# Four load buffers for three modulation vectors, and a rest in the steps that build the first gate

## The chip, the cores and the metric

The kernel runs on one core of a Trainium2 chip. The metric is the device time of one execution in microseconds (us); less is better. The engines are named as in the profile: PE (matrix engine), PEld (its weight loads), DVE (vector), ACT (scalar), POOL (GpSimd) and SP, whose queue issues every load of this kernel.

## The reference, cut to what matters

The kernel is one decoder layer for 512 tokens of width 1024: a modulated norm, an input projection, two groups of attention heads, an output projection, and an MLP. Six vectors of 1024 numbers modulate it:

```
mod = c @ w_ada + b_ada
sh1, sc1, gt1, sh2, sc2, gt2 = split(mod, 6)
h = rms_norm(x, g_pre_mix) * (1 + sc1) + sh1
o = attention(h @ w_in) @ w_out
x = x + gt1 * rms_norm(o, g_post_mix)
h = rms_norm(x, g_pre_ffn) * (1 + sc2) + sh2
x = x + gt2 * rms_norm(square(relu(h @ w_up)) @ w_down, g_post_ffn)
```

The change concerns gt1 (in the kernel the first gate, tiles `wv_g1`, `vs_g1`), sc2 (`a2`) and sh2 (`sh2`). Each is a vector of 1024 times a 1024 by 1024 block of `w_ada`, 4 MB. The trace leaves digits out of names, so `wv_g` is `wv_g1` there. gt2 is made elsewhere, in another way.

## The kernel before, in words

The program is one stream of steps, fully unrolled. It first computes sh1 and sc1 from `w_ada` (tiles `wm`, `macc`) while the first two column blocks of the input projection run (`pA`, `pB`, to about 81 us of the trace). Then come the other projections in chunks D, C and E (`pj_D`, `pj_C`, `pj_E`), with rotation, stacking and transposing of each piece (`ra`, `sk`, `skp`), the indexer scores (`ix`, `rl`, `wk`), the rounds that pick the top keys on DVE (`topk_round`, L571), and the compressed keys (`kcp`, `hid`). After that twelve units of attention run with the output projection (`op`) between them, and from 387 us the MLP (`up`, `dn`).

Side work is placed by the table PLAN (L41): a list of steps with the entry (t0, dt) is spread evenly over the slots t0 to t0+dt, step q of n at t0 + (q+0.5)/n*dt. Slot n is written into the program behind the n-th piece of main work (L850), so the slot of a step fixes its rank. Piece n of the main work includes one chunk of the projection: C0 to C3 stand in pieces 9 to 12.

Rank is not the order on the engines. The framework's scheduler lays every engine's instructions out when the program is built: it plays the program through its own time model and lets an engine take a step of lower rank when those of higher rank aren't ready. A tile with a tag takes one of the tag's buffers and holds it until its last reader is done; a step whose buffer isn't free isn't ready. On the chip each engine, and SP's queue of loads, then works strictly in the order laid out.

`vec_steps` (L710) makes one vector: 8 loads of 512 KB (tag "vw", two buffers), 8 steps `mm(i)` on PE of four small matmuls each (the trace shows eight), and after every fourth a `finish`. A load needs the buffer that an earlier `mm` gives back. The four `mm` of one half add into one PSUM bank `vs`, held until `finish` has read it; banks of the tag "S" (four) also serve the projection's pieces and the indexer scores. For the first gate `finish` (L746) adds the bias tile `bb` on DVE, spreads it over the partitions on PE (`gv_g`) and multiplies on DVE. `bb` is one of six buffers of the tag "m2", which rotation, stacking and indexer tiles use too. Its result is first read by the output projection, in slot 25. The vectors a2 and sh2 have slots 25 to 27 and 29 to 32.

Of the kernel before, what the change touches and what calls it, by code (L numbers as in the profile page):

```python
# [9 lines left out]
F32 = mybir.dt.float32  # L10
# [7 lines left out]
P = 128  # L18
# [27 lines left out]
    x22=(32.6, 0.1), h22=(33.35, 1.68), x23=(33.6, 0.1), sD=(0, 0.48), cl=(0.2, 4.48), lC=(0.5, 0.1),  # L46
    sC=(3.7, 2.94), lE=(8.2, 0.1), sE=(8.3, 5.379), ix=(8.2, 5.88), cpe=(10, 0.1), ck1=(11.1, 1.077),
    cv1=(13.2, 0.784), ck2=(11.7, 2.8), ck3=(15, 2.8), cv2=(14.6, 0.98), cv3=(15.2, 1.05), tk1=(13, 6),
    g1=(6, 8),
)  # L50
UNITS = [("s", 0), ("w", 0), ("s", 1), ("w", 1), ("d", 0), ("d", 1),
         ("s", 2), ("w", 2), ("d", 2), ("s", 3), ("w", 3), ("d", 3)]
# [17 lines left out]
def layer_kernel(  # L70
# [6 lines left out]
    nc = tc.nc  # L77
# [3 lines left out]
    big = ctx.enter_context(tc.tile_pool(name="big", bufs=1))  # L81
    sml = ctx.enter_context(tc.tile_pool(name="sml", bufs=1))
    psp = ctx.enter_context(tc.tile_pool(name="psp", bufs=2, space=PSUM))

    N_U, N_RAW, N_B4, N_K, N_P, N_M = 10, 4, 9, 6, 7, 6

    def ht(tag, name, dt=F32R):
        return big.tile([P, NT, KT, P], dt, tag=tag, name=name, bufs=1)
# [16 lines left out]
    def m2(name, dt=F32):  # L105
        return big.tile([P, 512], dt, tag="m2", name=name, bufs=N_M)
# [5 lines left out]
    def bank(tag, name, dt=F32):  # L112
        return psp.tile([P, 512], dt, tag=tag, name=name, bufs=4 if tag == "S" else 2)
# [426 lines left out]
    def Q2(nm, t):  # L540
        rv = heads(pjs[nm, t], 8)
        sks[nm, t] = [stack(rv[:, g * 4:g * 4 + 4, :], 4, f"{nm}{t}{g}", G) for g in range(2)]

    def Q3(nm, t):
        q = b4(f"q{nm}_{t}", F32R).rearrange("p (h q) -> p h q", q=P)
        for g in range(2):
            ps = stack_T(sks[nm, t][g], 4, f"{nm}{t}{g}")
            A.copy(q[:, g * 4:g * 4 + 4, :], ps.rearrange("p (h q) -> p h q", q=P))
        (qn if nm == "C" else qd)[t] = q
# [113 lines left out]
    none = lambda *a: None  # L663
# [43 lines left out]
                V.scalar_tensor_tensor(acc[:, sl], ps, ROOT_D, gb[:, sl], op0=OP.mult, op1=OP.mult)  # L707
        return seq + [fin]

    def vec_steps(c0, nm, finish):  # L710

        stt = {}

        def load(i):
            stt[i] = big.tile([P, 4, 256], F32, tag="vw", name=f"wv_{nm}{i}", bufs=2)
            n, q = divmod(i, 2)
            SY.dma_start(stt[i], wa[:, 4 * q:4 * q + 4, c0 + n * 256:c0 + n * 256 + 256])

        def mm(i):
            half, n, q = i // 4, i // 2 % 2, i % 2  # L720
            if i % 4 == 0:
                stt["ps"] = bank("S", f"vs_{nm}{half}")
            for j in range(4):
                PE.matmul(stt["ps"][32 * j:32 * j + 32, n * 256:n * 256 + 256],
                          c_sb[:, 4 * q + j:4 * q + j + 1].to_broadcast([P, 32]), stt[i][:, j, :],
                          start=(q == 0), stop=(q == 1))
            if i % 4 == 3:
                finish(half, stt["ps"])
        nv = 2
        seq = [lambda i=i: load(i) for i in range(nv)] + [none] * 6  # L730
        for i in range(8):
            seq.append(lambda i=i: mm(i))
            if i + nv < 8:
                seq.append(lambda i=i: load(i + nv))
        return seq

    def g1_steps(c0, gvec):
        bb = {}

        def begin():  # L740
            res["g1"] = big.tile([P, 1024], F32, tag="g1", name="g1", bufs=1)
            SY.dma_start(res["g1"], gvec.to_broadcast([P, D]))
            for half in range(2):
                bb[half] = m2(f"bb_{half}")
                SY.dma_start(bb[half], b_ada[0:1, c0 + half * 512:c0 + half * 512 + 512].to_broadcast([P, 512]))

        def finish(half, ps):
            g = res["g1"][:, half * 512:half * 512 + 512]
            V.scalar_tensor_tensor(bb[half], bb[half], 0.25, ps, op0=OP.mult, op1=OP.add)
            pg = bank("S", f"gv_g1{half}")  # L750
            PE.matmul(pg, ones, bb[half], start=True, stop=True)
            V.tensor_tensor(g, pg, g, op=OP.mult)
        return [begin] + vec_steps(c0, "g1", finish)

    def col_steps(c0, nm):
        dst = cst.tile([P, KT], F32, name="col_" + nm)

        def finish(half, ps):
            acc = m2(f"acc_{nm}{half}")
            A.copy(acc, ps)  # L760
            pc = bank("S", f"cv_{nm}{half}")
            for k in range(4):
                PE.matmul(pc[:, k:k + 1], acc[:, k * P:(k + 1) * P], ones[:, 0:1], start=True, stop=True)
            h = half * 4
            V.scalar_tensor_tensor(dst[:, h:h + 4], pc[:, 0:4], 1.0 / 32.0,
                                   colT[:, c0 // P + h:c0 // P + h + 4], op0=OP.mult, op1=OP.add)
        return dst, vec_steps(c0, nm, finish)
# [19 lines left out]
    for f in lD:  # L787
# [4 lines left out]
            lambda t, nm=nm: Q2(nm, t), lambda t, nm=nm: Q3(nm, t)), t) for t in range(NT) for nm in "C"]  # L792
    tl += tD + tC
    ix = [(t, h) for t in range(1, NT) for h in range(4)]
    tk = {t: topk_steps(t) for t in range(1, NT)}
    g1s = g1_steps(2 * D, g_post_mix)
    a2, a2s = col_steps(4 * D, "a2")
    sh2, sh2s = col_steps(3 * D, "sh2")
# [39 lines left out]
    for n in range(len(tl) + 3):  # L838
# [5 lines left out]
        while mm_done < min(want, len(mm_seq)):  # L844
            f, t = tl[mm_seq[mm_done]]
# [290 lines left out]
    def finish(t, half):  # L1136
        hs = [slice(i * 512, i * 512 + 512) for i in range(2)]
        jk = m2(f"fj_{t}{half}")
        A.activation(jk, yacc[t][:, hs[half]], AF.Square, accum_out=sy[t][:, half:half + 1])  # L1139
        V.tensor_tensor(yacc[t][:, hs[half]], yacc[t][:, hs[half]], res["g2"][:, hs[half]], op=OP.mult)  # L1140
        if half == 1:
            rs = st([P, 1], "ro")
            rstd_of(rs, sy[t])
            for i in range(2):
                V.scalar_tensor_tensor(yacc[t][:, hs[i]], yacc[t][:, hs[i]], rs, x2[t][:, hs[i]],
                                         op0=OP.mult, op1=OP.add)
                SY.dma_start(ov[t][:, hs[i]], yacc[t][:, hs[i]])
# [58 lines left out]
```

## Time and profile before

| what | us |
|---|---|
| median of 3 runs | 737.91 |
| lowest and highest of them | 736.64, 738.00 |
| the profiled execution's own time | 736.85 |
| its span, first to last instruction | 735.1 |

The span is what the trace covers; 1.75 us lie around it. Row times count from the start of the span. A wait in brackets is the idle time of that engine just before the row, with what ended it. PEclk, the granted clock, has two levels: 1.00 is 2.4 GHz and 0.50 is 1.2 GHz; over a stretch it is a mean.

### The profile page before, as it was taken

How to read it: one execution, taken by the hardware profiler on the slowest of the kernel's cores; microseconds unless marked ns; L12 is line 12 of the kernel's file. 1: busy time of each engine (PE TensorE's matmuls, PEld its weight loads, DVE VectorE, ACT ScalarE, POOL GpSimd, SP SyncE). 2: the span in 40 equal slices, each digit the busy share in tenths (PEclk: the TensorE clock that was granted, in tenths of full speed). 3: DMA queues.
4: the chain of work that ended last, by engine and by line, in shares of the span. 5: the costliest groups of instructions: out<-in, count | busy, mean ns of one | idle time of the engine just before them, and what ended most of it. 6: DMA issues, size and time to landing. Idle time of an engine off the chain costs nothing.

```text
span 735.1 us, 9839 instructions
## 1 busy us (share of the span) xinstructions
PE 686.9 (93%) x3473; PEld 541.7 (74%) x3473; DVE 485.3 (66%) x1014; ACT 341.8 (46%) x715; POOL 160.5 (22%) x223
## 2 busy tenths in 40 slices
PE   3878997999999999899999999999999999999995
PEld 2656885777766576565698888888888888788884
DVE  5997644979999988885586464653735445443547
ACT  6654584624788569554475313322331332323222
POOL 4673084535623243321020000000000000000003
PEclk9998998969979999999999999999999999999998
DMA  8985643170004580462131352533325133231202
GB/s 268 325 267 151 190 112 119 57 173 1 2 1 132 164 221 8 135 230 83 51 98 58 98 168 107 160 127 115 126 65 183 58 114 115 78 123 58 86 1 114
DMA packets 67610, 87.13 MB, mean 119 GB/s; under 512 B 3973, under 2 KB 38889, under 8 KB 67562
## 3 DMA queue, kind: packets, MB, share of 16 engines
q1 hardware_dynamic: 67562, 86.52, 38.0%
q8 instruction: 27, 0.44, 0.2%
q14 instruction: 21, 0.17, 0.1%
HBM read 84.40 MB, written 2.10 MB: 118 GB/s over the span
## 4 chain that ended last, share of the span: by engine, by line
PE 75%; DVE 14%; DMA 3%; issue 3%; ACT 2%; POOL 1%; SPq 0%; POOLq 0%; DVEq 0%; ACTq 0%
PE up L1119 23%; PE dn L1160 22%; PE op L1012 6%; PE O L911 3%; PE pj_E L323 2%; DVE macc L289 2%; PE pA L323 2%; PE pj_D L323 2%; PE pj_C L323 2%; PE tp_s L905 1%; DMA x<-in_x_dram 1%; PE pB L323 1%; PE tp_w L905 1%; PE hid_v L628 1%; DMA wv_g<-in_w_ada_dram 1%
## 5 line engine op out<-in xcount | busy, mean ns | idle before, releaser
L1119 PE MATMUL up<-hh,uh_U 128*128 128x512 f32 (+1 forms) x288 | 104.6, 366 | 0.7 <-ACT hh L123 0.7
L1119 PE MATMUL up<-hh,ul_U 128*128 128x512 f32 (+1 forms) x288 | 104.9, 366 | 0.0
L1119 PE MATMUL up<-hl,uh_U 128*128 128x512 f32 (+1 forms) x288 | 104.0, 366 | 0.0
L1160 PE MATMUL dn<-uh_D,al 128*128 128x512 f32 x256 | 99.6, 389 | 0.0
L1160 PE MATMUL dn<-uh_D,ah 128*128 128x512 f32 x256 | 98.7, 391 | 0.0
L1160 PE MATMUL dn<-ul_D,ah 128*128 128x512 f32 x256 | 98.5, 389 | 0.0
L203 POOL TENSOR_SCALAR ms<-sy 128x1 f32<-128x1 f32 x4 | 3.6, 911 | 341.6 <-ACT fj L1139 341.6
L124 DVE TENSOR_TENSOR ul_D<-rw_D,uh_D 128x1024 fp32r<-128x1024 f32 (+1 forms) x35 | 41.3, 1181 | 47.5 <-ACT uh_D L123 45.4
L1166 DVE TENSOR_TENSOR y<-dn,y 128x512 f32<-128x512 f32 x56 | 38.3, 689 | 50.3 <-PE dn L1160 50.3
L1123 ACT ACTIVATE rl<-up 128x512 f32<-128x512 f32 x32 | 19.1, 598 | 92.7 <-PE dn L1160 59.2
L1119 PEld LDWEIGHTS up<-hh,uh_U 128*128 128x128 f32 x288 | 54.3, 188 | 9.7 <-ACT hh L123 0.9
L1119 PEld LDWEIGHTS up<-hh,ul_U 128*128 128x128 f32 x288 | 54.3, 189 | 8.8
L1119 PEld LDWEIGHTS up<-hl,uh_U 128*128 128x128 f32 x288 | 53.7, 189 | 8.9 <-DVE hl L124 0.2
L123 ACT CAST uh_U<-rw_U 128x1024 fp32r<-128x1024 f32 x32 | 33.7, 1052 | 55.1 <-PE dn L1160 51.9
L123 ACT CAST uh_D<-rw_D 128x1024 fp32r<-128x1024 f32 (+1 forms) x36 | 36.3, 1010 | 49.5 <-PE up L1119 37.5
L1160 PEld LDWEIGHTS dn<-uh_D,al 128*128 128x128 f32 x256 | 48.1, 188 | 10.2 <-issue 0.2
L1160 PEld LDWEIGHTS dn<-uh_D,ah 128*128 128x128 f32 x256 | 48.0, 188 | 10.2 <-issue 0.2
L1160 PEld LDWEIGHTS dn<-ul_D,ah 128*128 128x128 f32 x256 | 48.0, 188 | 10.0
L124 DVE TENSOR_TENSOR ul_U<-rw_U,uh_U 128x1024 fp32r<-128x1024 f32 x32 | 39.1, 1222 | 11.9 <-ACT uh_U L123 10.9
L1124 DVE TENSOR_TENSOR rl<-rl 128x512 f32<-128x512 f32 x32 | 22.1, 690 | 34.8 <-ACT rl L1123 34.8
L123 ACT CAST ah<-rl 128x512 fp32r<-128x512 f32 x32 | 19.8, 620 | 29.3 <-DVE rl L1124 29.3
L124 DVE TENSOR_TENSOR al<-rl,ah 128x512 fp32r<-128x512 f32 x32 | 22.0, 689 | 11.0 <-ACT ah L123 11.0
(409 smaller groups left out, 1558.7 us busy)
## 6 DMA issues: line engine op xcount, KB each, us to landing
rw_U<-in_w_up_dram SPq DMA_DIRECT2D x32, 512.0 KB, 4.7
rw_D<-in_w_down_dram SPq DMA_DIRECT2D x32, 512.0 KB, 3.5
wm<-in_w_ada_dram SPq DMA_DIRECT2D x32, 256.0 KB, 5.3
wv_g<-in_w_ada_dram SPq DMA_DIRECT2D x8, 512.0 KB, 6.9
rwo_a<-in_w_out_dram SPq DMA_DIRECT2D x16, 256.0 KB, 4.4
wv_a<-in_w_ada_dram SPq DMA_DIRECT2D x8, 512.0 KB, 4.6
rwo_b<-in_w_out_dram SPq DMA_DIRECT2D x16, 256.0 KB, 4.0
wv_sh<-in_w_ada_dram SPq DMA_DIRECT2D x8, 512.0 KB, 5.1
```

Source lines behind the costliest of these rows:

```text
L123: A.copy(hi, src)
L124: eng.tensor_tensor(lo, src, hi.bitcast(F32), op=OP.subtract)
L289: steps.append(lambda i=i: V.scalar_tensor_tensor(acc[:, 0], sl[i], c_sb[:, i:i + 1], acc[:, 0], op0=OP.mult, op1=OP.add))
L323: PE.matmul(ps[:, :n], l[:, t, k, :], r[:, k % 2, :n], start=(k == 0 and i == 0), stop=(k == KT - 1 and i == 2))
L905: PE.transpose(tp[:, i * P:(i + 1) * P], self.P[g * 4 + i][:, kb * P:(kb + 1) * P], ident)
L911: mm = [PE.matmul(O[j][g * 64:(g + 1) * 64, :], vn[kb][:, self.vsl[g]:self.vsl[g] + 64], pts[kb, g][0], start=(first and kb == 0), stop=(l ...
L1012: PE.matmul(stt["ps"], l[:, kk, :], r[:, kk % 2, :], start=(kk == 0 and i == 0), stop=(kk == 7 and i == 2))
L1119: PE.matmul(pv[:, t0:t1, :], l[:, k % 2, fs], r[:, t0:t1, k, :], start=(n == 0), stop=(n == 23))
L1123: A.activation(rl, ps, AF.Relu)
L1124: V.tensor_tensor(rl, rl, rl, op=OP.mult)
L1160: PE.matmul(ps, l[:, t * P:(t + 1) * P], r[:, f % 2, :], start=(n == 0), stop=(n == 11))
L1166: V.tensor_tensor(ya, ps, ya, op=OP.add)
```

## The change

Loads of the three vectors (one shared tag) get four buffers. In `vec_steps` four loads stand ahead of the six empty steps instead of two, and each of the first four `mm` is followed by the load four places on. For the first gate ten empty steps are put behind the fourth `mm` and the load after it, and its list is spread over slots 6 to 18 instead of 6 to 14. The program reserves 1024 bytes of each partition for descriptors of DMAs made by software, in place of the default.

```
-    g1=(6, 8),
+    g1=(6, 12),
...
-    N_U, N_RAW, N_B4, N_K, N_P, N_M = 10, 4, 9, 6, 7, 6
+    N_U, N_RAW, N_B4, N_K, N_P, N_M, N_V = 10, 4, 9, 6, 7, 6, 4
...
-    def vec_steps(c0, nm, finish):
+    def vec_steps(c0, nm, finish, rest=0):
...
-            stt[i] = big.tile([P, 4, 256], F32, tag="vw", name=f"wv_{nm}{i}", bufs=2)
+            stt[i] = big.tile([P, 4, 256], F32, tag="vw", name=f"wv_{nm}{i}", bufs=N_V)
...
-        nv = 2
-        seq = [lambda i=i: load(i) for i in range(nv)] + [none] * 6
+        seq = [lambda i=i: load(i) for i in range(N_V)] + [none] * 6
         for i in range(8):
             seq.append(lambda i=i: mm(i))
-            if i + nv < 8:
-                seq.append(lambda i=i: load(i + nv))
+            if i + N_V < 8:
+                seq.append(lambda i=i: load(i + N_V))
+            if i == 3:
+                seq += [none] * rest
...
-        return [begin] + vec_steps(c0, "g1", finish)
+        return [begin] + vec_steps(c0, "g1", finish, 10)
...
-    nc = _bacc.Bacc("TRN2", target_bir_lowering=False, num_devices=1)
+    nc = _bacc.Bacc("TRN2", target_bir_lowering=False, num_devices=1, dynamic_dma_scratch_size=1024)
```

## Rows read from the trace of the kernel before

**Rows 1.** Page: busy us, share of the span, instructions, by engine.
```profile
PE 686.9 (93%) x3473; PEld 541.7 (74%) x3473; DVE 485.3 (66%) x1014; ACT 341.8 (46%) x715; POOL 160.5 (22%) x223
```

**Rows 2.** Chain that ended last, 100 to 165: start, us, what.
```profile
107.61 7.10 DMA wv_g<-in_w_ada_dram
...
117.44 7.50 PE pj_C L323 x24
```

**Rows 3.** Timeline of PE, 109.2 to 122.3: start, us, instruction, idle before.
```profile
110.30 0.28 PE L559 MATMUL ix<-k2a,qi 128*128 128x256 f32 x1
113.41 0.64 PE L724 MATMUL vs_g<-wv_g,c_sb 128*32 128x256 f32 x8 [2.84 <-DMA wv_g<-in_w_ada_dram]
...
114.75 1.08 PE L724 MATMUL vs_g<-wv_g,c_sb 128*32 128x256 f32 x8 [0.41 <-DMA wv_g<-in_w_ada_dram]
116.64 0.58 PE L558 MATMUL ix<-k1a,qi 128*128 128x256 f32 x1 [0.81 <-DVE bb L749]
...
117.24 0.63 PE L323 MATMUL pj_C<-uh_C,hh 128*128 128x512 f32 x1
...
121.78 0.39 PE L323 MATMUL pj_C<-uh_C,hl 128*128 128x512 f32 x1
122.01 0.40 PE L323 MATMUL pj_C<-uh_C,hh 128*128 128x512 f32 x1
```

**Rows 4.** Stretches: length, busy of PE, PEld, DVE, ACT, POOL, then PEclk, DMA share, GB/s.
```profile
114.80:121.60 6.80, 5.99 (x21) 4.14 (x22) 4.95 (x14) 2.23 (x7) 1.91 (x5) 0.50 0.51 157
148.90:162.50 13.60, 13.60 (x57) 11.06 (x58) 9.27 (x28) 2.29 (x5) 2.27 (x4) 0.50 0.83 196
```

**Rows 5.** Timeline of DVE, 109 to 126.
```profile
115.90 0.69 DVE L749 SCALAR_TENSOR_TENSOR bb<-bb,vs_g 128x512 f32<-128x512 f32 x1 [5.80 <-PE vs_g L724]
...
116.71 0.35 DVE L563 TENSOR_SCALAR wk<-rl,wi 128x256 f32<-128x256 f32 x1
...
125.26 0.17 DVE L606 COPY peT<-pep_k 128x16 f32<-128x16 f32 x1 [2.50 <-PE pep_k L604]
```

**Rows 6.** Timeline of ACT, 113 to 115.
```profile
113.73 0.38 ACT L561 ACTIVATE rl<-ix 128x256 f32<-128x256 f32 x1
```

**Rows 7.** Stretches behind that, columns as in Rows 4.
```profile
125.30:150.00 24.70, 22.77 (x134) 17.77 (x135) 24.04 (x62) 15.94 (x36) 14.73 (x18) 0.98 0.27 74
165.00:185.00 20.00, 19.23 (x116) 16.11 (x114) 19.21 (x72) 10.40 (x33) 9.76 (x14) 1.00 0.01 1
185.00:260.00 75.00, 71.03 (x424) 49.81 (x424) 74.43 (x252) 56.51 (x161) 29.73 (x41) 0.91 0.28 85
```

**Rows 8.** Timeline of SP's queue, 0 to 200: start, us, issue, count.
```profile
32.13 1.26 SPq L717 DMA_DIRECT2D wv_g<-in_w_ada_dram  x2
...
107.14 9.12 SPq L717 DMA_DIRECT2D wv_g<-in_w_ada_dram  x4
142.02 0.72 SPq L994 DMA_DIRECT2D rwo_a<-in_w_out_dram  x1
142.85 0.52 SPq L717 DMA_DIRECT2D wv_g<-in_w_ada_dram  x1
```

**Rows 9.** Timeline of PE, 140.5 to 154.8.
```profile
140.95 0.64 PE L724 MATMUL vs_g<-wv_g,c_sb 128*32 128x256 f32 x8
...
147.01 0.64 PE L724 MATMUL vs_g<-wv_g,c_sb 128*32 128x256 f32 x8 [0.70 <-DMA wv_g<-in_w_ada_dram]
148.87 4.53 PE L628 MATMUL hid_v<-kcp_v,w_v 128*128 128x62 f32 x20 [1.23 <-DVE kcp_v L618]
...
153.57 1.08 PE L724 MATMUL vs_g<-wv_g,c_sb 128*32 128x256 f32 x8
```

**Rows 10.** A stretch of the first stage, columns as in Rows 4.
```profile
20.00:40.00 20.00, 17.54 (x67) 14.48 (x68) 19.07 (x31) 13.84 (x26) 13.73 (x13) 1.00 1.06 326
```

**Rows 11.** Waits of the readers of `wm`, 20 to 60: who ended them, us, times.
```profile
  DMA wm<-in_w_ada_dram: 0.7, 2
```

**Rows 12.** Who waited for `wv_sh`: us, times.
```profile
  PEld vs_sh L724: 1.0, 1
```

## The prediction

> **What bounds the kernel now.** I read the page first. PE is busy for 93% of the span [rows 1], so over the whole run the kernel is bound by PE, but a share says nothing about one stage. So I took the chain that ended last, in order of time, and looked for pieces that are neither PE nor DVE at work. Near the first gate there is one: a load of `wv_g` stands on the chain for 7.10 us, and a chunk of projection C comes right behind it [rows 2]. PE's timeline of that stretch shows what this load does [rows 3]. PE ends an indexer matmul at 110.58 and is idle until 113.41, waits for the next load until 114.75, and waits once more, for 0.81 us, until DVE has read the bank `vs` (the bias row `bb`). The projection matmuls that could have filled these waits stand behind, and an engine doesn't overtake its own queue. Then the stretches: behind the wait the granted clock is 0.50 from 114.8 to 121.6 [rows 4], so the work that follows the wait is slow too. DVE waits with PE: 5.80 us for `vs` and 2.50 us for a small transpose behind the chunk [rows 5]. From 125.3 on DVE is the bound: busy for 24.04 of 24.70 us, 19.21 of 20 and 74.43 of 75, with one stretch between in which PE is the bound at half clock [rows 4, 7]. What is gained at 125 therefore moves DVE's whole queue ahead, if nothing behind it comes at a fixed time. No load does: those that are late there wait for buffers which computation gives back.
>
> **Why the load is late.** The first two loads of the gate are issued at 32.1, more than 70 us before they are used. The next four go out from 107.14 on, when PE has given back the first buffers [rows 8]. The third is then used at 113.41, 6.27 us after it was issued, beside loads of projection E and of the bias.
>
> A rule of the Trainium skill speaks against this part. "DMA: Bandwidth & Descriptors", section "Anatomy of one DMA — SWDGE (gpsimd) path", gives one transfer about 2 us plus its bytes over 436 GB/s. An estimate from that page is 3.2 us for 512 KB: the third load would land at 110.3, just before PE gets to it, two buffers would do, and the time would stay at 737.9. The trace doesn't agree: here a load takes 6.27 and 7.10 us, and the measurement decides.
>
> **The change part by part.** *Four buffers, first half.* All four loads of the first half now need nothing from PE, so the first two waits have no cause: 2.84 + 0.41 = 3.25 us of PE [rows 3]. With PE kept busy I expect no half clock behind them. Eleven matmuls of the chunk take 121.78 - 117.24 = 4.54 us there; at the full clock they start 0.23 us apart [rows 3], so 2.53 us, which saves 2.01. The second group of `vs_g` takes 1.08 against 0.64 us for the same eight matmuls just before, 0.44 more. PE's side gives 3.25 + 2.01 + 0.44 = 5.7 us, and 0.8 more if the wait for `bb` goes as well.
>
> DVE's side is the tighter. Its indexer row at 116.71 needs the ACT row that ends at 113.73 + 0.38 = 114.11 [rows 5, 6], and ACT's queue is full ahead of it, so DVE can start it at most 2.6 us earlier. The wait of 2.50 us for the transpose goes too, since the chunk ahead of it ends over 5 us earlier. Together 5.1 us. I take the smaller, 5.1, because DVE is the bound behind. Bounds: 2.6 (only one of the two DVE waits goes) and 6.5 (PE's side with the third wait).
>
> *More slots and the rest.* Before, 23 steps lay over 8 slots: `mm` 0 to 3 at 9.3, 10.0, 10.7 and 11.4, the last four at 12.1 to 13.8. Now 33 steps lie over 12 slots: the first four at 10.2 to 12.4, the last four at 16.7 to 17.8. The first half thus ranks behind chunk C1 (piece 10) instead of before it, which can only help C1. The second half leaves 140.95 to 154.65 [rows 9]. Slot 14.6 holds `hid_v`, which starts at 148.87; slots 16 and 17 come behind it, and I take 165 to 185 for them. Where it goes from: the last group runs on PE's path at half clock, 1.08 us saved; the wait of 0.70 us ahead of the third is hidden, as PE then waits for DVE's `kcp_v` anyway. Where it goes to: four groups of 0.64 us are 2.6 us, and from 165 to 185 PE has 0.77 us free [rows 7], so up to 1.8 us are added. The bias row and the product on DVE only move. I take 0 for the part; bounds -1.1 and +1.8.
>
> *SP's queue.* Loads 4 to 7 of the gate now need only `mm` 0 to 3, so they may go out by about 120. Before, the loads of the output weights `rwo_a` blocked SP until 142.02, and a gate load stood behind them [rows 8]. What the first loads of a2 are moved behind is `mm` 4 to 7: they go out later, and so do the `rwo_a` loads queued after them. Both are used from slot 25 on, so the work of the seven slots between covers it. 0; if that cover were gone, one load's 6.27 us.
>
> *Two loads more in the first stage.* SP will issue them where it issued the first two, at 33. DMA is full there, 326 GB/s [rows 10], so 1.05 MB push what is behind by 3.2 us. That costs nothing if the `wm` parts have slack: their readers waited 0.7 us in all for these loads [rows 11], and DVE, busy for 19.07 of 20 us, is what sets the pace. 0; bound +3.2.
>
> *a2 and sh2.* Both are filler between output projection and attention. PE's queue waited 1.0 us for `wv_sh` [rows 12]. I take 0; bounds -1.0 and 0. *The descriptor reserve* is not used: every load goes out on SP's hardware queue. 0.
>
> **Sum.** -5.1 + 0 + 0 + 0 + 0. The profiled execution's 736.85 becomes 731.75. The median of the runs is 1.06 above that execution, so 732.8. Its own range adds the bounds that can meet: down by 1.4 (third wait), 1.1 and 1.0, up by 2.5 and 1.8, which is 729.3 to 737.1.
>
> **The rivals.** *More than that.* The half clock from 148.9 to 162.5 follows a stretch in which PE waits for a gate load and for DVE [rows 4, 9]. With the gate's groups gone the order there changes, and the stretch may run at the full clock. DVE has 13.60 - 9.27 = 4.3 us free in it, so at most 4.3 us more: 728.5. Against it: the wait for `kcp_v` remains, and there is less small work to fill PE.
>
> *Nothing comes of it.* The two early loads delay the first stage by their full 3.2 us, and the late groups cost their 1.8 us: 5.0 us back, 737.8. For it: DMA is full at 33, and 165 to 185 is full on both engines. Against it: the waits on `wm` are short. The skill's load time above, by which there was no wait to remove, gives the same time; the trace leaves it almost no chance, and it is counted here.
>
> *Slower: SP's queue.* The scheduler lays SP's queue anew. If a load of the gate's second half stands behind the first `rwo_a` load, it goes out at 142.85 - 5.1 = 137.75 and lands 4.2 us later (142.85 to 147.01 before [rows 8, 9]), at 141.9. If PE's queue has the group where it had the fifth, at 140.95 - 5.1 = 135.85, PE waits 6.1 us and then runs at half clock for 2.45 us of lost work as above: 8.5 - 5.1 = 3.4 us slower, 741.3. It decides from a wait of about 2.7 us on. For it: one such queue place already cost the first half its wait, and SP was blocked for 26 us in just this stretch. Against it: before, loads that needed `mm` 0 to 3 all went ahead of `rwo_a`, and the rest puts the second half four slots later.
>
> **How the numbers follow.** The forecast has 0.58, more than that 0.09, nothing 0.14, slower 0.19. The point is 732.8. Leaving out about one in ten on either side, from the lower rival to the upper, gives 727.5 to 741. About 0.2%, 1.5 us, is what a measurement of this kernel can tell from no change; faster by more than that has 0.58 + 0.09, less 0.01 for the end of the forecast's range: 0.66. Same 0.15, slower 0.19.
>
> **What would show it.** Right: four `wv_g` loads issued before 60; no wait for `wv_g` on PE between 100 and 120 and a granted clock of 1.00 there; `peT` on DVE about 5 us earlier, with DVE's queue behind it shifted by as much; the MLP, which now runs from 387, starting about 5 us earlier. Wrong: the first stage ending later than 81; a wait for `wv_g` at another place; a longer stretch of half clock between 140 and 185; or a shift at 125 that is gone by 200 because of a new order.

## The result, and the profile after

| | median, us | lowest and highest | runs |
|---|---|---|---|
| before | 737.27 | 736.57, 738.00 | 4 |
| after | 745.37 | 745.20, 748.09 | 4 |

The ratio is 1.0098, 95% interval 1.0071 to 1.0125: the change makes the kernel 8.1 us slower. The forecast was 732.8 with a range up to 741.0, so sign and range are both wrong. The profiled execution of after took 748.09 us, its span is 746.4, and its lines behind L730 are one higher than before. Single executions of before took from 735.55 to 743.34 us in the jobs below, and traces with the order of before lie 0.6 to 2.5 us behind it by 126, so a shift between two profiles is read only where it is larger, or where it is counted from a matmul that both have in the same place. One execution below, 752.72 us of `places_only`, was in the slower state and is left out of its median and ratio.

First the page's busy times by engine, against [rows 1]. PE's share is the same 93%, and its busy time has grown by 4.8 us.

```profile
PE 691.7 (93%) x3473; PEld 544.5 (73%) x3473; DVE 489.2 (66%) x1014; ACT 342.4 (46%) x715; POOL 160.3 (21%) x223
```

The place that the change is about. SP's queue, against [rows 8]: four gate loads go out together at 34, four more at 122 and later, all before the first `rwo_a`.

```profile
34.16 2.96 SPq L717 DMA_DIRECT2D wv_g<-in_w_ada_dram  x4
...
121.80 10.61 SPq L717 DMA_DIRECT2D wv_g<-in_w_ada_dram  x4
141.37 4.94 SPq L995 DMA_DIRECT2D rwo_a<-in_w_out_dram  x6
```

PE's timeline behind 108, against [rows 3]. No row waits for `wv_g`. But PE still stands idle here, 3.46 us, for an ACT row `rl`.

```profile
112.56 0.80 PE L323 MATMUL pj_C<-uh_C,hh 128*128 128x512 f32 x1 [3.46 <-ACT rl L561]
...
121.09 0.64 PE L724 MATMUL vs_g<-wv_g,c_sb 128*32 128x256 f32 x8
```

The stretches of after, columns as in [rows 4]. The half clock has not gone: the granted clock is 0.66 from 109 to 119 and 0.52 from 148.5 to 158.

```profile
109.10:119.00 9.90, 6.44 (x17) 5.11 (x18) 5.90 (x17) 4.77 (x15) 4.68 (x13) 0.66 0.00 0
148.50:158.00 9.50, 9.46 (x40) 8.33 (x41) 9.03 (x20) 2.50 (x6) 6.75 (x10) 0.52 0.86 266
```

DVE's timeline, against the last row of [rows 5]: `peT` starts at 121.20 instead of 125.26. So 4.06 us are gained here, and the forecast had 5.1. But 1.84 of them were there by the end of the first stage, before any matmul of the gate (last `pB` ends at 79.18, before at 81.02).

```profile
121.20 0.18 DVE L606 COPY peT<-pep_k 128x16 f32<-128x16 f32 x1 [1.16 <-PE pep_k L604]
```

That first gain is no scatter. From the same matmul of `pA`, near 56, to the last `pB` it is 24.70 us before and 21.75 after; in the seven kernels with four buffers it is 20.6 to 21.8, in the seven with two 24.7 to 25.8. PE's, DVE's and POOL's timelines of before show what goes: three products on DVE take 4.63 us beside POOL's splits, where in after each takes 0.48; `ulA` stands behind them on DVE, and PE waits 2.77 us for it.

```profile
70.42 1.88 PE L323 MATMUL pA<-ulA,hh 128*128 128x452 f32 x4 [2.77 <-DVE ulA L124]
```
```profile
64.72 4.63 DVE L289 SCALAR_TENSOR_TENSOR macc<-wm,c_sb,macc 128x256 f32<-128x256 f32 x3
```
```profile
65.17 1.41 POOL L124 TENSOR_TENSOR ul_D<-rw_D,uh_D 128x560 fp32r<-128x560 f32 x1 [3.65 <-ACT uh_D L123]
66.53 2.55 POOL L124 TENSOR_TENSOR ulB<-rwB,uhB 128x1024 fp32r<-128x1024 f32 x1
```

All seven traces with two buffers have that wait, 2.77 to 2.79 us, and none of the seven with four. The seven with four all have the new descriptor reserve too, so the runs don't tell the buffers from it. From the end of that stage to `peT` the gain is 2.2 us in after and 2.0 to 2.8 in the others with four buffers.

Where the time is lost shows in the landmarks of three traces, in us from the span's start. `gate_list` is an experiment below.

| PE | before | after | gate_list |
|---|---|---|---|
| last `pj_E` ends | 195.10 | 190.99 | 189.99 |
| first `op` (output projection) starts | 225.53 | 227.46 | 226.39 |
| first `vs_sh` starts | 313.64 | 316.53 | 314.76 |
| last `vs_sh` ends | 351.02 | 360.38 | 350.33 |
| last `op` ends | 372.06 | 377.61 | 373.79 |
| last `hp` (transposes for the MLP's input) ends | 386.10 | 397.83 | 387.86 |
| last `dn` ends | 726.72 | 737.95 | 728.47 |

There are two losses. From 191 to 227 a lead of 4.1 us turns into a lag of 1.9. From 317 to 398 a lag of 2.9 grows to 11.7. Behind that nothing changes: from the last `hp` to the last `dn` it is 340.6 us before and 340.1 after. In neither stretch does a step of the gate run.

The first loss, by DVE's, POOL's and PE's timelines of after. DVE runs six small products `P_d`. In the kernel before they take 1.33 us, and POOL's split `uol_a` comes behind them; here they take 3.44. One of the six, normally 0.27 us long, starts just behind `uol_a` and ends with it. The row maxima `mx` stand behind it on DVE, and PE waits 2.98 us for them; from 224.4 to 227.0 the granted clock is 0.50. First before, DVE and POOL, then after. This is only a part of the loss: the same stretch, from the last `pj_E` to the first `op`, takes 30.4 us before and 36.5 after, but also 32.7 in gate4_plain and 35.3 in four_only (below), which have no such wait.

```profile
220.79 1.33 DVE L900 TENSOR_SCALAR P_d<-P_d,rs 128x128 f32<-128x128 f32 x6
```
```profile
223.71 2.41 POOL L124 TENSOR_TENSOR uol_a<-rwo_a,uoh_a 128x1024 fp32r<-128x1024 f32 x1 [2.65 <-ACT uoh_a L123]
```
```profile
219.97 3.44 DVE L901 TENSOR_SCALAR P_d<-P_d,rs 128x128 f32<-128x128 f32 x6
```
```profile
220.98 2.35 POOL L124 TENSOR_TENSOR uol_a<-rwo_a,uoh_a 128x1024 fp32r<-128x1024 f32 x1 [0.72 <-ACT uoh_a L123]
```
```profile
224.40 0.58 PE L880 MATMUL s_d<-k1a,qE 128*128 128x256 f32 x1 [2.98 <-DVE mx L883]
```

The second loss, by PE's timeline of after. The second half of sh2 (`vs_sh`) runs from 349 to 360; the first `hp` comes at 368.79, 8.8 us before the last `op` ends; before, it came at 357.41, 14.65 us ahead of that end. So part of the work that makes the MLP's input no longer has output projection beside it to fill PE. PE waits for it, and behind it the granted clock is 0.80 from 375 to 385. First before, then after:

```profile
349.95 1.07 PE L724 MATMUL vs_sh<-wv_sh,c_sb 128*32 128x256 f32 x16
...
357.41 0.66 PE L1054 MATMUL hp<-ident,xn 128*128 128x128 f32 x4
```

```profile
353.89 1.06 PE L724 MATMUL vs_sh<-wv_sh,c_sb 128*32 128x256 f32 x12
...
359.74 0.64 PE L724 MATMUL vs_sh<-wv_sh,c_sb 128*32 128x256 f32 x8
...
368.79 0.60 PE L1055 MATMUL hp<-ident,xn 128*128 128x128 f32 x4
...
379.04 0.63 PE L1055 MATMUL hp<-ident,xn 128*128 128x128 f32 x4 [0.99 <-DVE xn L1052]
381.53 0.58 PE L1120 MATMUL up<-hh,uh_U 128*128 128x256 f32 x1 [1.86 <-ACT hh L123]
```
```profile
375.00:385.00 10.00, 7.15 (x36) 6.20 (x36) 9.15 (x18) 8.16 (x20) 2.22 (x4) 0.80 0.51 157
```

### The profile page after: what moved, and what is told of

Same layout as the page of the kernel before. It is cut to its first block, busy times and chain, and to the rows that moved or that the text cites. A ratio compares the mean times of both kernels' runs of the same rounds, so it can differ in the third digit from the quotient of the medians.

```text
span 746.4 us, 9842 instructions
## 1 busy us (share of the span) xinstructions
PE 691.7 (93%) x3473; PEld 544.5 (73%) x3473; DVE 489.2 (66%) x1014; ACT 342.4 (46%) x715; POOL 160.3 (21%) x223
## 4 chain that ended last, share of the span: by engine, by line
PE 76%; DVE 14%; ACT 3%; DMA 3%; issue 2%; SPq 1%; POOL 1%; DVEq 0%; POOLq 0%; ACTq 0%
PE up L1120 24%; PE dn L1161 22%; PE op L1013 6%; PE pj_C L323 3%; PE O L912 3%; PE pj_E L323 2%; PE pj_D L323 2%; DVE macc L289 1%; DVE wk L576 1%; DMA x<-in_x_dram 1%; PE pA L323 1%; DVE m L573 1%; PE hid_v L628 1%; PE tp_s L906 1%; DVE P_d L901 1%
## 5 line engine op out<-in xcount | busy, mean ns | idle before, releaser
L1120 PE MATMUL up<-hh,uh_U 128*128 128x512 f32 (+1 forms) x288 | 106.2, 371 | 1.9 <-ACT hh L123 1.9
L124 DVE TENSOR_TENSOR ul_D<-rw_D,uh_D 128x1024 fp32r<-128x1024 f32 (+1 forms) x35 | 44.0, 1259 | 49.3 <-ACT uh_D L123 47.3
L1161 PEld LDWEIGHTS dn<-uh_D,ah 128*128 128x128 f32 x256 | 48.1, 188 | 10.2 <-issue 0.2
L1161 PEld LDWEIGHTS dn<-uh_D,al 128*128 128x128 f32 x256 | 48.1, 188 | 10.2 <-issue 0.2
L124 DVE TENSOR_TENSOR al<-rl,ah 128x512 fp32r<-128x512 f32 x32 | 22.1, 689 | 11.7 <-ACT ah L123 11.7
```

Of the source, the lines that this page charges most:

```text
L124: eng.tensor_tensor(lo, src, hi.bitcast(F32), op=OP.subtract)
L1120: PE.matmul(pv[:, t0:t1, :], l[:, k % 2, fs], r[:, t0:t1, k, :], start=(n == 0), stop=(n == 23))
L1161: PE.matmul(ps, l[:, t * P:(t + 1) * P], r[:, f % 2, :], start=(n == 0), stop=(n == 11))
```

## The experiments

Three theories stood at the start. *Order*: every edit makes the scheduler lay out much of the program anew, and the time follows from where the steps fall, not from the loads. *Rest*: the ten empty steps and the wider spread of the gate cost it. *a2 and sh2*: their longer lead, which the same edit brings, delays sh2 and leaves the tail of h2 bare. Twelve kernels ran. Ratios are to the kernel before in the same job.

| kernel | median, us | ratio | 95% interval |
|---|---|---|---|
| four_only | 738.11 | 1.0007 | 0.9979 to 1.0036 |
| rest_only | 734.27 | 0.9948 | 0.9909 to 0.9986 |
| gate_list | 737.96 | 1.0001 | 0.9983 to 1.0019 |
| nudge_t0 | 741.47 | 1.0038 | 1.0017 to 1.0058 |
| gate4_plain | 729.15 | 0.9871 | 0.9852 to 0.9890 |
| gate4_places | 735.21 | 0.9947 | 0.9926 to 0.9969 |
| places_only | 742.77 | 1.0065 | 1.0034 to 1.0095 |
| sh2_two | 737.32 | 0.9984 | 0.9965 to 1.0002 |
| gate4_nudge | 737.14 | 0.9982 | 0.9965 to 0.9998 |
| sh2_fourth | 743.85 | 1.0078 | 1.0060 to 1.0096 |
| nudge_tk2 | 741.76 | 1.0051 | 1.0035 to 1.0067 |
| nudge_early | 742.90 | 1.0059 | 1.0038 to 1.0079 |

**four_only**: the change without rest and spread.

```
-    g1=(6, 12),
+    g1=(6, 8),
...
-        return [begin] + vec_steps(c0, "g1", finish, 10)
+        return [begin] + vec_steps(c0, "g1", finish)
```

> Four buffers and lists four ahead for all three vectors, but the gate's list keeps slots 6 to 14 and has no rest. Theory 'order' (each edit makes the scheduler lay out the attention anew, and the new layouts are worse by some us wherever they differ): the wait on the gate's loads near 107 is gone, the time is anything from 735 to 748, and the loss, if there is one, is at steps that were not edited. Theory 'rest' (the rest and the spread over 12 slots cost the time): 733, four us under the kernel before. Theory 'a2 and sh2' (their longer lead ends sh2 later and leaves the tail of h2 bare): 742 to 746, with the loss behind 305 alone.

Between the theories: as fast as before, 7 us faster than the change. Its last `pj_E` ends at 182.07, 13 us ahead of before, and 7 of that still stand at the first `vs_sh` (306.81). At the last `vs_sh` (350.70) the lead is gone.

**rest_only**: before, with the rest and the spread alone.

```
-    g1=(6, 8),
+    g1=(6, 12),
...
+            if i == 3:
+                seq += [none] * rest
...
-        return [begin] + vec_steps(c0, "g1", finish)
+        return [begin] + vec_steps(c0, "g1", finish, 10)
```

> Two buffers as before; only the gate's list has the ten empty steps and lies over 12 slots. Theory 'rest': the loss of 196 to 228 (6 us in the changed kernel) is here too, 742 to 745. Theory 'order': anything from 735 to 748, with the wait on the gate's loads still there or moved. Theory 'a2 and sh2': no loss behind 305; 737, as before.

It is 0.5% faster than before, just below every value expected. So the rest has no price of its own: with two buffers it gains about 4 us. PE still waits 2.45 us for `wv_g` here, at 113.7, and yet `peT` comes at 115.97, 9.3 us earlier than before: where the steps fall sets that time as much as the load does.

**gate_list**: the change, with the lists of a2 and sh2 two loads ahead.

```
-        seq = [lambda i=i: load(i) for i in range(N_V)] + [none] * 6
+        seq = [lambda i=i: load(i) for i in range(ahead)] + [none] * 6
...
-        return dst, vec_steps(c0, nm, finish)
+        return dst, vec_steps(c0, nm, finish, ahead=2)
```

> The changed kernel, except that the lists of a2 and sh2 stay two loads ahead. Its PE order is that of the changed kernel up to the third attention pair, near 235, so up to there it must show the same times (+2.4 us at 230 against the kernel before). Theory 'a2 and sh2': the loss from 305 on, 9 us, goes, and the time is 736 to 737. Theory 'order': the part behind 235 is a new layout, neither that of before nor that of the change, and the time is anything from 736 to 750. Theory 'rest': 745, as the changed kernel.

As the theory of a2 and sh2 has it for the second loss: the ratio is 1. Up to 235 the first 1051 matmuls of its trace come in the same sequence as those of after, 1.05 us earlier at that point, and they show the first loss too. Then the orders part, and at the last `hp` it is 10.0 us. So 8.9 us were lost behind, by the lists of a2 and sh2 alone (these traces are 9.5 us apart, the medians 7.4).

**nudge_t0**: before, with one number changed.

```
-    g1=(6, 8),
+    g1=(6.1, 8),
```

> The kernel before with one number changed: the gate's list begins at slot 6.1 instead of 6. The same steps, buffers and loads; some steps change places with a neighbour. Theory 'order': the time moves by more than 2 us, to either side, by differences in stretches far from the gate. Both other theories: 737 to 738, as before.

0.38% slower, 2.8 us: what is no change in work, buffers or loads costs a third of what the whole change costs. That speaks for order.

**gate4_plain**: four_only, with the lists of a2 and sh2 two loads ahead.

> four_only with the lists of a2 and sh2 two loads ahead again: four buffers, the gate's list four ahead in its old slots 6 to 14, no rest. In four_only the trace was 13 us ahead at the end of projection E, 7 to 8 at 230 and level with the kernel before at 351. If the steps of a2 and sh2 cost what they cost in the changed kernel (7 us between 305 and 398), and nothing else eats the lead, this kernel ends at 730 to 732. If the lead is lost to whatever order the scheduler makes of the rest, 736 to 740.

729.15, 1.3% faster than before and the fastest of all kernels here. With four_only, gate_list and after it makes a square:

| ratio to before | a2, sh2 two ahead | a2, sh2 four ahead |
|---|---|---|
| gate four ahead, slots 6 to 14 | 0.9871 | 1.0007 |
| the same, rest, slots 6 to 18 | 1.0001 | 1.0098 |

On 737.3 us the first column says that four buffers and early loads for the gate alone are worth -9.5, and that rest and spread then cost 9.6; the second row, that the lists of a2 and sh2 cost 7.2. Where the first two part shows in the traces of gate4_plain and gate_list. On DVE the second sum `kcp_v` comes 3.55 us earlier in gate4_plain. First gate4_plain, then gate_list:

```profile
143.21 0.68 DVE L618 TENSOR_TENSOR kcp_v<-kcp_v,peT 128x512 f32<-128x512 f32 x1
```
```profile
146.76 0.67 DVE L618 TENSOR_TENSOR kcp_v<-kcp_v,peT 128x512 f32<-128x512 f32 x1
```

PE of gate4_plain has the four last groups of the gate between other work and goes on to `hid_v` with no wait. PE of gate_list has them in one block and then waits. Both timelines:

```profile
138.37 0.64 PE L724 MATMUL vs_g<-wv_g,c_sb 128*32 128x256 f32 x8
...
143.94 0.64 PE L724 MATMUL vs_g<-wv_g,c_sb 128*32 128x256 f32 x8
...
144.71 2.04 PE L628 MATMUL hid_v<-kcp_v,w_v 128*128 128x62 f32 x16
```
```profile
143.29 1.93 PE L724 MATMUL vs_g<-wv_g,c_sb 128*32 128x256 f32 x32
145.16 0.54 PE L423 MATMUL skp_C<-identr,sk_C 128*128 128x128 f32 x4
147.49 3.47 PE L628 MATMUL hid_v<-kcp_v,w_v 128*128 128x62 f32 x16 [1.79 <-DVE kcp_v L618]
```

The stretch behind, again gate4_plain first, has a granted clock of 1.00 in one and 0.51 in the other:

```profile
147.50:158.00 10.50, 10.42 (x56) 8.51 (x55) 10.40 (x28) 2.95 (x8) 5.93 (x10) 1.00 0.68 181
```
```profile
147.50:158.00 10.50, 10.50 (x42) 9.18 (x43) 10.02 (x21) 2.98 (x7) 7.51 (x12) 0.51 0.89 266
```

In gate4_plain PE also has no wait of 2.98 us near 221.

**gate4_places**: four buffers and four early loads for the gate, but every matmul step at its old place in the list; a2 and sh2 as before.

```
+            seq = [lambda i=i: load(i) for i in range(4)] + [none] * 4
+            for i in range(8):
+                seq.append(lambda i=i: mm(i))
+                if i < 6:
+                    seq.append((lambda i=i: load(i + 4)) if i < 4 else none)
```

> Four buffers, and the gate's first four loads stand ahead, but each of its eight matmul steps keeps the place in the list that it has in the kernel before (four empty steps ahead of the first instead of six); a2 and sh2 as before. So this is the removed wait alone. By the forecast's sum (5.1 us of DVE's queue at 125 move the whole rest) 732 to 733. If a lead of DVE is worth nothing where PE becomes the bound (from about 228 on), 736 to 739, with a lead on DVE at 190 that is gone at 230 on PE.

735.21 lies between the two: by the ratio 3.9 us are gained where the sum had 5.1. But this isn't the removed wait alone, as the expectation has it: of the lead of 6.9 us at `peT` (118.36), 4.2 stand at the end of the first stage (last `pB` ends at 76.84), so 2.7 come from the stretch in which the wait went. The lead is 5.2 at the end of `pj_E` (189.93), 2.9 at the first `op` (222.68), and 3.2 at the end; which part of it is left there, the run doesn't show.

**places_only**: the reverse. Two buffers, loads two ahead, and only the matmul steps of a2 and sh2 at the places that the change gives them.

```
+            seq = [lambda: load(0), lambda: load(1)] + [none] * 8
+            for i in range(4):
+                seq += [lambda i=i: mm(i), lambda i=i: load(i + 2)]
+            for i in (4, 5):
+                seq.append(lambda i=i: (mm(i), load(i + 2)))
```

> The kernel before, two buffers and loads two ahead throughout; only the matmul steps of a2 and sh2 are put at the places in their lists that they have in the changed kernel (the first four two places later, the fifth and sixth two and one). No load is more or less ahead, no wait is removed. If the places cost the time: 743 to 745, with the second half of sh2 and h2 as late as in the changed kernel (first hp 8 us ahead of the last op instead of 14). If the buffers or the earlier loads cost it: 737 to 738.

742.77: the places cost, without a buffer or an early load. But the trace isn't as expected: its first `hp` still stands 14.6 us ahead of the last `op`, and it is 1.9 us late by 235, where its order parts from that of before, and 5.7 at the last `op` (377.71 against 372.06). The same places cost some 4 us here by another way: 3.0 of them are lost between 235 and the first `vs_sh` (318.56), and 0.7 from there to the last `hp`. Yet sh2's second half is drawn out here too, to 363.14.

**sh2_two**: the change, with sh2's list alone two ahead (`ahead=2 if nm == "sh2" else 4`).

> The changed kernel with sh2's list alone two loads ahead; a2 and the gate as in the change. If it is sh2's fourth matmul step (with the reading of its bank behind it) that matters, as it goes from slot 30.98 to 31.25 and so behind one more attention pair: 737 to 739, as gate_list. If it is a2, whose steps stay within their slots: 744 to 746, as the changed kernel.

737.32: it is sh2. a2's steps cost nothing here that can be measured. The expectation has them within their slots, but one isn't: a2's list has 23 steps over slots 25 to 27, and its second matmul step goes from 25 + 10.5/23 x 2 = 25.91 to 25 + 12.5/23 x 2 = 26.09. So a border that is passed need not cost.

**sh2_fourth**: before, with one step of sh2's list moved.

```
+        if behind:
+            late = seq[14:17]
+            seq[14:17] = [none, none, lambda: [f() for f in late]]
```

> The kernel before with one step moved: in sh2's list alone the fourth matmul step, with the reading of its bank and the load behind it, goes from place 14 to place 16, that is from slot 30.98 to 31.25. If passing this border (one attention pair more ahead of it) is what the change paid for: 742 to 744, as places_only, with the first hp some 8 us ahead of the last op. If not: 737 to 739.

743.85, with the first `hp` 10 us ahead of the last `op` (364.86 and 374.82). One step that passes the border of slot 31 costs 0.78%, 5.8 us (a load moves with it, within slot 31). The nudges of before cost up to 4.4, but elsewhere: the first 1583 matmuls of this trace come in the sequence of before, 0.9 us late at 330, and at the last `hp` (392.10) it is 6.0. PE's timeline of this kernel shows the pattern of after: sh2's second half drawn out to 360, then waits among `hp` and `up`.

```profile
350.14 0.64 PE L724 MATMUL vs_sh<-wv_sh,c_sb 128*32 128x256 f32 x8
...
356.20 0.64 PE L724 MATMUL vs_sh<-wv_sh,c_sb 128*32 128x256 f32 x8
...
359.80 0.63 PE L724 MATMUL vs_sh<-wv_sh,c_sb 128*32 128x256 f32 x6
...
364.86 0.60 PE L1057 MATMUL hp<-ident,xn 128*128 128x128 f32 x4
...
391.47 0.63 PE L1057 MATMUL hp<-ident,xn 128*128 128x128 f32 x4 [0.99 <-ACT hq L1065]
393.07 0.39 PE L1122 MATMUL up<-hh,uh_U 128*128 128x256 f32 x1 [0.97 <-ACT hh L123]
```

Over all fourteen traces, the second loss goes with a late `hp`. Where the first `hp` starts 14.6 us ahead of the end of the last `op`, in eleven, it is 71.9 to 74.4 us from the first `vs_sh` to the last `hp`. In after, four_only and sh2_fourth the first `hp` is 8.8, 8.8 and 10.0 us ahead, and it is 81.3, 81.1 and 77.4.

**gate4_nudge**: gate4_plain, with `g1=(6.1, 8)`.

> gate4_plain with one number changed: the gate's list begins at slot 6.1 instead of 6. No rest, no wider spread. The order that comes of it differs from that of gate_list, the kernel with rest and spread, in 17 of 3240 PE instructions, and from that of gate4_plain in 112. If the rest as such costs time: 729 to 731, as gate4_plain. If it is only the order into which the steps fall: 736 to 739, as gate_list, with the second half-sum kcp_v on DVE at 146 to 147 and a half clock on PE behind it.

737.14: a tenth of a slot takes 8.2 of the 9.5 us away, with no rest in it. The second `kcp_v` is on DVE at 148.00, PE waits 0.98 us for it, and the wait for `mx` is back, as PE's timeline shows. The half clock that was expected behind `kcp_v` isn't there (1.00 from 147.5 to 158), so that part was wrong.

```profile
148.72 3.67 PE L628 MATMUL hid_v<-kcp_v,w_v 128*128 128x62 f32 x30 [0.98 <-DVE kcp_v L618]
...
222.20 0.39 PE L878 MATMUL s_d<-k1a,qE 128*128 128x256 f32 x1 [2.98 <-DVE mx L881]
```

**nudge_tk2** and **nudge_early**: before, with `tk2=(17.9, 3.5)` and with `g1=(5.9, 8)`.

> The kernel before with the list of the second top-key rounds begun at slot 17.9 instead of 17.8. The gate, its loads, a2 and sh2 aren't touched. By the theory that any new layout costs time in the stretch that the old one was fitted to: 738.5 to 743, and more than 16.4 us from the first score of the first d unit to the first op. Otherwise 737 to 738.

> The kernel before with the gate's list begun at slot 5.9 instead of 6. By the theory that any new layout costs time: 738.5 to 743, as begun at 6.1. By the theory that the time follows the place of the gate (later is worse): 735 to 737.

Both are slower, by 0.51 and 0.59%. In nudge_tk2 the stretch named in the expectation is 16.7 us, no more than before's within what a profile can tell. It is 1.9 us late at 161, where its order parts from that of before, and 4.9 at the first `vs_sh` (318.60); nudge_early is 0.8 ahead at the first `op` (224.73) and 4.4 late at the first `vs_sh` (318.03). What costs it in between stays open. Begun at 5.9 or at 6.1, the kernel is slower than at 6, so it isn't a matter of earlier or later.

## Why the prediction was wrong

**The failed step is "a2 and sh2: 0 (-1.0 and 0)".** It priced the waits for their loads (1.0 us) and left out that the same edit puts two loads more ahead of the six empty steps, and so every matmul step of the first half two places further back. The sum was done for the gate (10.2 to 12.4 instead of 9.3 to 11.4) and not for sh2, though the table allows it: 22 steps over slots 29 to 32, the fourth at place 14 before and 16 now, 29 + 14.5/22 x 3 = 30.98 and 29 + 16.5/22 x 3 = 31.25. It passes the border of a slot, and work of the next piece of attention comes ahead of it. Shown: with sh2's list put back the change costs nothing (sh2_two, gate_list); this one step by itself costs 5.8 us (sh2_fourth). The term is +7.2 instead of 0, outside its bounds, and it is almost the whole result. Not shown is that the border as such costs: a2 passes one for nothing (sh2_two), and in places_only the same step at the same place loses 0.7 us in sh2's stretch. What goes with the loss is the late first `hp`.

**"More slots and the rest: 0 (-1.1 to +1.8)" is off by more than its range, but not by what it described.** The second half did not go to 165 to 185; its matmuls had ended at 146.26, where before they ended at 154.65 [rows 9]. With four buffers the rest costs 9.6 us, with two it gains about 4, and a tenth of a slot costs as much as the rest does. So among these kernels it decided the layout that the scheduler falls into: one in which `kcp_v` is ready when PE gets there and no `mx` stands behind POOL's split, and one in which both go wrong. That order alone has such a price is shown by gate4_nudge, which pays 8.2 with no rest in it; that these two waits are the whole of the price is not shown.

**The removed wait.** That the loads were late for want of buffers, and that four would end the wait, is right: no PE row waits for `wv_g`. But the term of -5.1 is too large: from the end of the first stage to `peT` after gains 2.2 us, just under the lower bound of 2.6, and gate4_places 2.7. Two parts of the forecast's picture are wrong. PE did not stay busy there: with the wait for loads gone a wait for ACT is next, 3.46 us up to 112.56, and the half clock stays. The sum had let ACT's `rl` [rows 6] bound DVE; PE waits for a row of the same line. And "what is gained at 125 moves DVE's whole queue ahead" holds to about 190 and not beyond: in 190 to 230 after loses what it had.

**The other steps.** SP's queue: right, no gate load stood behind `rwo_a`, and the slower rival by that mechanism did not occur. The slower side came by another way. Two loads more in the first stage: 0 was wrong. It cost nothing, as argued, but the new order there gains about 3 us in after (24.70 to 21.75), and the forecast had no term for that. The load time of the Trainium skill ("DMA: Bandwidth & Descriptors", section "Anatomy of one DMA — SWDGE (gpsimd) path"), by which there was no wait to remove, did not decide. The gate's loads go out on SP's queue, not on GpSimd's path, and took 4.1 to 8.4 us from issue to landing in before; the wait was there, and its removal has the measured worth above. The rival *more than that* (the half clock from 148.9 goes, 728.5) did not happen in the change, but it did in gate4_plain: that stretch has the clock 1.00 and the time is 729.15. It needed `kcp_v` early, which the rival had named as what spoke against it. That the time comes within 0.7 us of the rival's is luck: some 3 us of it were gained in the first stage, of which the rival says nothing.

**The size of the parts.** Along one way through the square they are -9.5 (the gate's buffers and loads, the first stage with them), +9.6 (rest and spread), +7.2 (the lists of a2 and sh2). Taken the other way, those lists come first with 0.0136 x 737.3 = 10.0 and the rest then costs 6.7. So the sizes depend on each other by 3 us; within the square the signs don't. The wording of the forecast's last line, "a shift at 125 that is gone by 200 because of a new order", was the right warning; it had no price and no chance in the sum.

What stays open: why the new order for sh2 draws its second half out (in after its eight loads are all issued by 320.5, and none is waited for, so it isn't they) and in three kernels puts `hp` late; whether the first stage gains by the buffers or by the descriptor reserve; and whether `uol_a` placed elsewhere on POOL would remove the wait at 221 alone. An edit for it would move the order again, and it wasn't tried.

## What to carry to other kernels

In a program whose order a scheduler works out from ranks, an edit of a helper moves every list that the helper makes: work out the new rank of each step of each caller, and look above all for steps that pass a border; whether such a step costs, only a run tells. Before such a change is judged, measure how far the time moves under nudges that change no work: here a tenth of a slot is worth 2.8 to 8 us, as much as the wait that was to be removed. And take such a change apart: the part that was wanted was worth -9.5 us, some 3 of them from a stage that the forecast had at 0, and two riders cost 16.8.

## What the runs showed of the hardware

A DVE instruction can be held for the whole length of one on POOL. In after a `tensor_scalar` of 128 by 128, 0.27 to 0.37 us long in its five neighbours, starts at 221.05, 0.07 us after POOL's `uol_a`, and ends at 223.42, 0.09 us after it. The Trainium skill, "SBUF — State Buffer", section "Who interferes with whom", says that the two engines share a pair of ports as an exclusive lock, and that beside a DVE instruction in a mode that uses both of its ports the engine that issues second blocks fully for the whole instruction; it names `tensor_scalar` among those that can run so. The trace agrees on the holdup; no row shows the mode. The number of such holdups is no measure of the damage: up to 400 us, DVE instructions that take over 0.35 us more than the median of their kind (same line, names and shape) number 33 in before and 32 in after. What counts is what stands behind the held instruction: in after the row maxima that PE waited 2.98 us for, in before `ulA`, 2.77 us.
